# An encoder's feed-forward layers: gate and up by Strassen's seven block products, down in three parts

## The chip, the core and the metric

The kernel runs on one NeuronCore of a Trainium2 chip. PE (TensorE) multiplies matrices: it loads a 128x128 block of the stationary operand (PEld in the profile) and streams the columns of the moving operand through it into one of eight PSUM banks of 128 x 512 floats. DVE (VectorE), ACT (ScalarE) and POOL (GpSimd) work on tiles of 128 partitions; SP issues the DMA transfers from the chip's memory. Each engine takes its own instructions in order and waits for the others by semaphores. The metric is the device time of one execution in microseconds (us).

## The reference

The program is a two-layer encoder trunk on 512 tokens of width 1024, in float32. Layer 0 mixes tokens by neighbourhood attention and a bidirectional state-space scan, layer 1 by grouped-query attention. After each mixer stands a feed-forward network with hidden width 2816, and that is the part which the change touches:

```
def rms_norm(x, g):
    xf = x.astype(jnp.float32)
    y = xf * lax.rsqrt(jnp.mean(xf * xf, axis=-1, keepdims=True) + NORM_EPS)
    return (y * g.astype(jnp.float32)).astype(x.dtype)

def swiglu_ffn(x, norm_g, w13, w2):
    g, u = jnp.split(rms_norm(x, norm_g) @ w13, 2, axis=-1)
    return (jax.nn.silu(g) * u) @ w2
```

The result is added to x. The columns of w13 are 2816 for the gate g and 2816 for u (up); w2 leads back (down).

## The kernel before

The residual stream is kept transposed in eight tiles res[0..7] of 128 features x 512 tokens. A product in float32 quality is made of three fast ones: each operand is split into hi (a copy in the reduced type float32r, by ScalarE) and lo (the remainder t - hi, by VectorE), and mm3 (L150 to L155) adds lo*hi, hi*lo and hi*hi into one PSUM bank. So each 128x128 block of weights costs three matmuls of 512 columns, each with its own weight load.

load_w (L138 to L148) brings a weight tile of 128 x 1024: a DMA into a raw buffer (two, tag wr), a ScalarE copy to hi, a VectorE subtraction to lo (three buffers each, tags wh and wl). project (L166) multiplies one such tile with the eight input blocks: 24 matmuls. prep (L171) makes hi and lo of res[k] times the norm's gain.

ffn (L773 to L808) runs for each layer after its mixer. Hidden features are worked in HB = 22 blocks of 128. For each block there are two projections, gate into bank gp and up into bank up, 48 matmuls. The norm's factor rstd for each token isn't needed before the products are read: it is made from squares of res (L770), a column sum by two matmuls (sum_rows, L131) and a chain of ScalarE and VectorE operations (L189 to L200), and is multiplied on when the bank is read (L790, L792). silu is taken by ScalarE, the product g*s by VectorE (L793), and the hidden block is split again into hi and lo (L795, L796); all 22 hidden pairs stay in SBUF. Down then makes the eight output blocks one after the other, each from 22 hidden blocks in one bank, with weights in three loads (8, 8 and 6 blocks), and adds it to res (L806). In layer 1 the sum leaves by DMA (L808).

PSUM: seven of the eight banks are handed out in turn for ffn (turns["f"]), one is left for sums. Working tiles of 128 x 512 come from a pool of NSLOT = 12 slots, the split inputs from a pool of 16 (xgslot).

The order of instructions is made by a planner, which takes dependences and its own estimates of durations; only in the first mixer is a stretch of PE's order written out by hand (manual_schedule with PE alone).

## Time and profile before

| | |
|---|---|
| median of 3 runs | 1314.04 us (1313.2 to 1314.28) |
| the profiled execution | 1314.37 us, its span 1312.6 us |
| granted clock of PE, mean | 0.996 |
| busy share of the span | PE 98%, weight loads 81%, DVE 61%, ACT 46%, POOL 13% |
| feed-forward matmuls | nine groups of 352, 128x128 by 128x512 |
| DMA | 138.82 MB, mean 106 GB/s |

The span goes from the first to the last instruction of the profiled execution; its own time includes what lies around it. A row of the timeline gives the start in us, the duration, the engine, the line, the operation with output and inputs, and in brackets how long the engine had been idle before and what released it. Matmuls are pipelined, so their durations overlap: the distance between starts is what one costs. A group's row ends with its count, busy time and mean duration in ns, and the idle time of the engine before its instructions.

### The profile page before, as it was taken

How to read it: one execution, taken by the hardware profiler on the slowest of the kernel's cores; microseconds unless marked ns; L12 is line 12 of the kernel's file. 1: busy time of each engine (PE TensorE's matmuls, PEld its weight loads, DVE VectorE, ACT ScalarE, POOL GpSimd, SP SyncE). 2: the span in 40 equal slices, each digit the busy share in tenths (PEclk: the TensorE clock that was granted, in tenths of full speed). 3: DMA queues.
4: the chain of work that ended last, by engine and by line, in shares of the span. 5: the costliest groups of instructions: out<-in, count | busy, mean ns of one | idle time of the engine just before them, and what ended most of it. 6: DMA issues, size and time to landing. Idle time of an engine off the chain costs nothing.

```text
span 1312.6 us, 16744 instructions
## 1 busy us (share of the span) xinstructions
PE 1288.4 (98%) x6278; PEld 1062.6 (81%) x6278; DVE 805.2 (61%) x1262; ACT 604.0 (46%) x1023; POOL 167.5 (13%) x184
## 2 busy tenths in 40 slices
PE   9999999989999999999999999999999999999998
PEld 7777788867888888888888878778888888888887
DVE  6798798989684444444332578998864444443221
ACT  7676567866363333332233348777743222222220
POOL 5012011102000000000011325655100000000000
PEclk9999999989999999999999999999999999999999
DMA  7334443536333333323333343221132333333331
GB/s 239 97 98 153 128 132 114 177 93 191 105 111 97 97 96 96 97 97 104 94 100 103 112 105 89 81 65 33 49 113 96 97 97 96 96 97 106 107 118 55
DMA packets 49761, 138.82 MB, mean 106 GB/s; under 512 B 6736, under 2 KB 7888, under 8 KB 49680
## 3 DMA queue, kind: packets, MB, share of 16 engines
q1 hardware_dynamic: 49392, 137.23, 34.5%
q8 instruction: 49, 0.80, 0.2%
q10 hardware_dynamic: 288, 0.52, 0.1%
q14 instruction: 32, 0.26, 0.1%
HBM read 127.11 MB, written 2.23 MB: 99 GB/s over the span
## 4 chain that ended last, share of the span: by engine, by line
PE 81%; DVE 12%; ACT 4%; issue 2%; DMA 1%; SPq 0%; POOL 0%; DVEq 0%; ACTq 0%; POOLq 0%
PE fo L155 6%; PE fo L154 6%; PE fo L153 6%; PE fu L153 6%; PE fu L155 6%; PE fu L154 6%; PE fg L155 6%; PE fg L154 6%; PE fg L153 6%; PE g L153 2%; PE g L154 2%; PE g L155 2%; PE vps L271 2%; PE opt L968 1%; PE oA L153 1%
## 5 line engine op out<-in xcount | busy, mean ns | idle before, releaser
L155 PE MATMUL fg<-f_xh,wfg_h 128*128 128x512 f32 x352 | 137.0, 389 | 0.0
L154 PE MATMUL fg<-f_xl,wfg_h 128*128 128x512 f32 x352 | 137.0, 389 | 0.0
L153 PE MATMUL fu<-f_xh,wfu_l 128*128 128x512 f32 x352 | 136.9, 389 | 0.0
L154 PE MATMUL fu<-f_xl,wfu_h 128*128 128x512 f32 x352 | 136.9, 389 | 0.0
L155 PE MATMUL fu<-f_xh,wfu_h 128*128 128x512 f32 x352 | 136.9, 389 | 0.0
L153 PE MATMUL fo<-hh,wf_l 128*128 128x512 f32 x352 | 136.9, 389 | 0.0
L154 PE MATMUL fo<-hl,wf_h 128*128 128x512 f32 x352 | 136.9, 389 | 0.0
L155 PE MATMUL fo<-hh,wf_h 128*128 128x512 f32 x352 | 136.9, 389 | 0.0
L153 PE MATMUL fg<-f_xh,wfg_l 128*128 128x512 f32 x352 | 136.9, 389 | 0.0
L146 ACT ACTIVATE wf_h<-wf_r 128x1024 fp32r<-128x1024 f32 (+1 forms) x48 | 47.5, 990 | 180.3 <-PE fo L155 158.2
L147 DVE TENSOR_TENSOR wf_l<-wf_r,wf_h 128x1024 fp32r<-128x1024 f32 (+1 forms) x48 | 54.5, 1136 | 122.2 <-ACT wf_h L146 122.2
L146 ACT ACTIVATE wfg_h<-wfg_r 128x1024 fp32r<-128x1024 f32 x44 | 46.6, 1060 | 142.3 <-issue 127.3
L146 ACT ACTIVATE wfu_h<-wfu_r 128x1024 fp32r<-128x1024 f32 x44 | 46.7, 1061 | 135.5 <-PE fg L155 129.4
L792 DVE TENSOR_TENSOR g<-fu,fr_r 128x512 f32<-128x512 f32 x44 | 30.4, 691 | 124.6 <-PE fu L155 123.4
L790 DVE TENSOR_TENSOR g<-fg,fr_r 128x512 f32<-128x512 f32 x44 | 30.2, 691 | 87.7 <-PE fg L155 87.6
L155 PEld LDWEIGHTS fg<-f_xh,wfg_h 128*128 128x128 f32 x352 | 66.2, 188 | 13.9
L154 PEld LDWEIGHTS fo<-hl,wf_h 128*128 128x128 f32 x352 | 66.1, 188 | 13.8
L154 PEld LDWEIGHTS fu<-f_xl,wfu_h 128*128 128x128 f32 x352 | 66.2, 188 | 13.7
L153 PEld LDWEIGHTS fu<-f_xh,wfu_l 128*128 128x128 f32 x352 | 66.1, 188 | 13.7
L154 PEld LDWEIGHTS fg<-f_xl,wfg_h 128*128 128x128 f32 x352 | 66.0, 188 | 13.8
L153 PEld LDWEIGHTS fo<-hh,wf_l 128*128 128x128 f32 x352 | 66.1, 188 | 13.7
L155 PEld LDWEIGHTS fu<-f_xh,wfu_h 128*128 128x128 f32 x352 | 66.0, 188 | 13.7
(421 smaller groups left out, 2997.0 us busy)
## 6 DMA issues: line engine op xcount, KB each, us to landing
wfg_r<-in_w_fa SPq DMA_DIRECT2D x44, 512.0 KB, 3.5
wfu_r<-in_w_fa SPq DMA_DIRECT2D x44, 512.0 KB, 3.5
wf_r<-in_w_fb SPq DMA_DIRECT2D x32, 512.0 KB, 3.5
w_r<-in_w_ssd SPq DMA_DIRECT2D x24, 512.0 KB, 3.5
wo_r<-in_w_o SPq DMA_DIRECT2D x14, 512.0 KB, 3.6
wf_r<-in_w_fb SPq DMA_DIRECT2D x16, 384.0 KB, 3.2
nb<-in_nab SPq DMA_DIRECT2D x16, 256.0 KB, 2.9
ec<-ecumd SPq DMA_DIRECT2D x32, 128.0 KB, 3.0
```

Of the source, the lines that this page charges most:

```text
L146: A.activation(hi[:, 0:cols], raw, AF.Copy)
L147: (eng or V).tensor_tensor(lo[:, 0:cols], raw, f(hi)[:, 0:cols], ALU.subtract)
L153: T.matmul(ps, wl[:, a], xh[:, b], start=first, stop=False)
L154: T.matmul(ps, wh[:, a], xl[:, b], start=False, stop=False)
L155: T.matmul(ps, wh[:, a], xh[:, b], start=False, stop=last)
L271: T.matmul(vps[t], x_, w_[:, ws_], start=k + n == 0, stop=k == KB - 1 and n == 2)
L790: V.tensor_tensor(g, gp, rstd, ALU.mult)
L792: V.tensor_tensor(g, up, rstd, ALU.mult)
L968: T.transpose(pt[:, a * 256 + n * P:a * 256 + (n + 1) * P], pr[n][:, (2 * kp + a) * P:(2 * kp + a + 1) * P], ident)
```

## The change

Only ffn, load_w and mm3 change, and with ffn the constants. In ffn, the first NCL = 4 hidden blocks are made as before (gate_up), and the other 18 by Strassen's scheme in Winograd's form, class Fast. The weights of one hidden block are four blocks (gate and up; first and second half of the 1024 input features), the input four blocks (halves of the features; halves of the tokens, H = 256). Instead of eight products of such blocks there are seven, each of 4 k-tiles x 3 matmuls with 256 columns:

- sums of weight blocks: s1 = up first + up second, s2 = s1 - gate first, s0 = gate first - up first, s3 = gate second - s2; each is split into hi and lo (w0 to w6);
- sums of input blocks, made once per layer by forms, from the input that is multiplied by gain and rstd beforehand: t12 and t34, beside the plain x1 and xb;
- the products are added up in three half banks pa, pb, pc, which are read in between: after the first, third and fourth product by a ScalarE copy, after the fifth and sixth by a VectorE addition. c11 and c12 make the silu of the two token halves, h0 and h1 split the hidden block.

run(prev, nxt) writes one round: the seven products, of which the second (p3) belongs to the block before, mixed with the finish of that block and with the weights of the next.

Down is cut along the hidden blocks into 0 to 4 (after the four plain blocks), 4 to 12 (after block 13) and 12 to 22 (at the end); each part adds to res. So hidden tiles can be reused. The remainder of a weight tile can be put off (los). The whole of ffn stands in manual_schedule for PE, DVE and ACT: these three keep the written order; DMA issues do not.

```diff
-W2_SPLIT = (8, 8, 6)
+NCL, MID, UA = 4, 13, 1
...
+        def low():
+            (eng or V).tensor_tensor(lo[:, 0:cols], raw, f(hi)[:, 0:cols], ALU.subtract)
+        if los is None:
+            low()
+        else:
+            los.append(low)
...
+        H = S // 2
+        LOH, HIH = slice(0, H), slice(H, S)
+        LW, HW = slice(0, S), slice(S, 2 * S)
...
+        def copy(dst, src, scale=1.0):
+            A.activation(dst, src, AF.Copy, scale=scale)
+        def rest(lo, t, hi):
+            V.tensor_tensor(lo, t, f(hi), ALU.subtract)
+        def pair_of(name, tag, bufs, cols=S):
+            return [hlane(f"{name}{n}{layer}", f"{tag}{n}", bufs, F32R, cols) for n in "hl"]
+        hb = [None] * HB
+        def hidden(i):
+            mk = (lambda name: hlane(name, "h", 8, F32R)) if i < NCL or 12 <= i < 16 else xgslot
+            hb[i] = [mk(f"h{n}{layer}_{i}") for n in "hl"]
+            return hb[i]
+        def load_fa(n, los=None):
+            return load_w(w_fa[layer, n], 1024, f"wf{layer}_{n}", los=los)
+        x1, xb, t12, t34 = [], [None] * 4, [None] * 4, [None] * 4
+        def forms(k, r):
+            n = f"{layer}_{k}"
+            xa, xc, ta, tb = (slot(f"{m}{n}") for m in ("xa", "xc", "ta", "tb"))
+            V.scalar_tensor_tensor(xa, res[k], vc(gname, k), r, ALU.mult, ALU.mult)
+            if k % 2 == 0:
+                x1.append(pair_of(f"xa{n}", "xa", 2))
+            cut = part(x1[k // 2], slice(k % 2 * H, k % 2 * H + H))
+            copy(cut[0], xa[:, LOH])
+            V.scalar_tensor_tensor(xc, res[k + 4], vc(gname, k + 4), r, ALU.mult, ALU.mult)
+            b4, t1, t3 = xb[k], t12[k], t34[k] = [pair_of(f"{m}{n}", m, 4) for m in ("xb", "ta", "tb")]
+            copy(b4[0], xc)
+            yield
+            V.tensor_tensor(ta[:, LOH], xa[:, HIH], xa[:, LOH], ALU.subtract)
+            V.tensor_tensor(ta[:, HIH], xc[:, HIH], ta[:, LOH], ALU.subtract)
+            copy(t1[0], ta)
+            yield
+            V.tensor_tensor(tb[:, LOH], xc[:, HIH], xa[:, HIH], ALU.subtract)
+            V.tensor_tensor(tb[:, HIH], xc[:, LOH], ta[:, HIH], ALU.subtract)
+            copy(t3[0], tb)
+            yield
+            rest(cut[1], xa[:, LOH], cut[0])
+            rest(b4[1], xc, b4[0])
+            rest(t1[1], ta, t1[0])
+            rest(t3[1], tb, t3[0])
+        def product(ps, w, x, first=False):
+            for k in range(4):
+                if x is x1:
+                    xs, xc = x1[k // 2], slice(k % 2 * H, k % 2 * H + H)
+                else:
+                    xs, xc = x[0][k], x[1]
+                mm3(ps, w, k * P, xs, xc, first and k == 0, k == 3, skip=True)
+        class Fast:
+            def __init__(self, i):
+                self.i, self.n = i, f"{layer}_{i}"
+            def load(self):
+                n = self.n
+                self.gr = wsp.tile([P, 1024], F32, name=f"gr{n}", tag="wr", bufs=WR)
+                self.ur = hlane(f"ur{n}", "ur", 2, F32, 1024)
+                nc.sync.dma_start(self.gr, w_fa[layer, 2 * self.i])
+                nc.sync.dma_start(self.ur, w_fa[layer, 2 * self.i + 1])
+            def w0(self):
+                n, gr, ur = self.n, self.gr, self.ur
+                self.wg = [wsp.tile([P, 1024], F32R, name=f"g{m}{n}", tag=f"w{m}", bufs=b)
+                           for m, b in (("h", WH), ("l", WL))]
+                self.s = [slot(f"s{m}{n}") for m in range(4)]
+                copy(self.wg[0], gr)
+                V.tensor_tensor(self.s[0], gr[:, LW], ur[:, LW], ALU.subtract)
+                V.tensor_tensor(self.s[1], ur[:, LW], ur[:, HW], ALU.add)
+            def w1(self):
+                V.tensor_tensor(self.s[2], self.s[1], self.gr[:, LW], ALU.subtract)
+                rest(self.wg[1], self.gr, self.wg[0])
+            def w2(self):
+                V.tensor_tensor(self.s[3], self.gr[:, HW], self.s[2], ALU.subtract)
+                self.w32 = pair_of(f"sa{self.n}", "ss", 3, 1024)
+                copy(self.w32[0][:, LW], self.s[0])
+                copy(self.w32[0][:, HW], self.s[2])
+            def w3(self):
+                rest(self.w32[1][:, LW], self.s[0], self.w32[0][:, LW])
+                rest(self.w32[1][:, HW], self.s[2], self.w32[0][:, HW])
+            def w4(self):
+                self.w14 = pair_of(f"sb{self.n}", "ss", 3, 1024)
+                copy(self.w14[0][:, LW], self.s[1])
+                copy(self.w14[0][:, HW], self.s[3])
+                rest(self.w14[1][:, LW], self.s[1], self.w14[0][:, LW])
+            def w5(self):
+                rest(self.w14[1][:, HW], self.s[3], self.w14[0][:, HW])
+            def w6(self):
+                self.wu = pair_of(f"ua{self.n}", "ua", UA)
+                split(self.ur[:, HW], *self.wu)
+            def p1(self):
+                n = self.n
+                self.pa, self.pb, self.pc = (fbank(f"f{m}{n}")[:, 0:H] for m in "abc")
+                self.a, self.b, self.u, self.g = (slot(f"{m}{n}") for m in ("sa", "sb", "up", "sl"))
+                product(self.pa, part(self.wg, LW), x1, True)
+            def c11(self):
+                V.tensor_tensor(self.b[:, HIH], self.pc, self.a[:, LOH], ALU.add)
+                A.activation(self.g[:, LOH], self.b[:, HIH], AF.Silu)
+            def p3(self):
+                product(self.pa, part(self.w14, HW), (xb, HIH))
+            def c12(self):
+                A.activation(self.g[:, HIH], self.pa, AF.Silu)
+                V.tensor_tensor(self.u, self.u, self.g, ALU.mult)
+            def h0(self):
+                copy(hidden(self.i)[0], self.u)
+            def h1(self):
+                rest(hb[self.i][1], self.u, hb[self.i][0])
+            def run(self, prev, nxt):
+                if prev:
+                    prev.c11()
+                if nxt:
+                    nxt.w0()
+                self.p1()
+                copy(self.a[:, LOH], self.pa)
+                if nxt:
+                    nxt.w1()
+                if prev:
+                    prev.p3()
+                    prev.c12()
+                if nxt:
+                    nxt.w2()
+                product(self.pb, part(self.w32, LW), (t34, LOH), True)
+                copy(self.b[:, LOH], self.pb)
+                if prev:
+                    prev.h0()
+                if nxt:
+                    nxt.w3()
+                if prev:
+                    prev.h1()
+                product(self.pa, part(self.w32, HW), (t12, HIH))
+                copy(self.a[:, HIH], self.pa)
+                if nxt:
+                    nxt.w4()
+                product(self.pb, self.wu, (t34, HIH))
+                V.tensor_tensor(self.u[:, LOH], self.pb, self.a[:, HIH], ALU.add)
+                if nxt:
+                    nxt.w5()
+                    nxt.w6()
+                product(self.pa, part(self.w14, LW), (t12, LOH))
+                V.tensor_tensor(self.u[:, HIH], self.pa, self.b[:, LOH], ALU.add)
+                product(self.pc, part(self.wg, HW), (xb, LOH), True)
+        class Down:
+            def __init__(self, lo, hi, splits, final=False, wide=1):
+                self.banks, self.blocks, self.ws, self.wide = {}, [], [], wide
+                for o in range(0, KB, wide):
+                    k0 = lo
+                    for j, n in enumerate(splits):
+                        self.blocks.append((o, j, k0, n))
+                        k0 += n
+                self.lo, self.hi, self.final, self.last = lo, hi, final, len(splits) - 1
+            def load(self, upto, los=None):
+                while len(self.ws) < min(upto, len(self.blocks)):
+                    o, j, k0, n = self.blocks[len(self.ws)]
+                    src = [w_fb[layer, o + e, :, k0 * P:(k0 + n) * P] for e in range(self.wide)]
+                    self.ws.append(load_w(src, self.wide * n * P, f"wf2{layer}_{o}_{self.lo}_{j}", los=los))
+            def add(self, m, o, ks):
+                o0, j, k0, n = self.blocks[m]
+                if o not in self.banks:
+                    self.banks[o] = fbank(f"fo{layer}_{o}_{self.lo}")
+                for k in ks:
+                    mm3(self.banks[o], self.ws[m], ((o - o0) * n + k - k0) * P, hb[k], ALL,
+                        k == self.lo, k == self.hi - 1)
+                if k == self.hi - 1:
+                    V.tensor_tensor(res[o], res[o], self.banks[o], ALU.add)
+                    if self.final and layer == 1:
+                        nc.sync.dma_start(out[o], res[o])
+            def run(self, side, head=0):
+                for m, (o0, j, k0, n) in enumerate(self.blocks):
+                    for fn in side.get(m, ()):
+                        fn()
+                    self.load(m + 2)
+                    for o in range(o0, o0 + self.wide):
+                        self.add(m, o, range(k0, k0 + n - (m < head)))
+                    if m + 1 == head:
+                        for e in range(head * self.wide):
+                            self.add(e // self.wide, e, [self.hi - 1])
+        def gate_up(i, ws, xg, tick):
+            for n in range(2):
+                ps = fbank(f"f{'gu'[n]}{layer}_{i}")
+                order = [(k, p) for k in range(KB) for p in range(3)]
+                if i + n == 0:
+                    order = [(k, p) for k in range(KB) for p in (0, 2)] + [(k, 1) for k in range(KB)]
+                for m, (k, p) in enumerate(order):
+                    (wh, wl), (xh, xl) = ws[n], xg[k]
+                    T.matmul(ps, (wl if p == 0 else wh)[:, k * P:k * P + P], xl if p == 1 else xh,
+                             start=m == 0, stop=m == 23)
+                tick(n, ps)
+        with tc.manual_schedule(engines={mybir.EngineType.PE, mybir.EngineType.DVE, mybir.EngineType.Activation}):
+            ws = [load_fa(0), load_fa(1)]
+            xg, sq = [], []
+            for k in range(KB):
+                xg.append(prep(res[k], vc(gname, k), f"f{layer}{k}"))
+            for k in range(KB):
+                sq.append(slot(f"f{layer}_sq{k}"))
+                A.activation(sq[k], res[k], AF.Square)
+            for k in range(1, KB):
+                V.tensor_tensor(sq[0], sq[0], sq[k], ALU.add)
+            rstd = []
+            late = []
+            down0 = Down(0, NCL, (NCL,), wide=2)
+            fast = [Fast(i) for i in range(NCL, HB)]
+            def norm():
+                name = f"fr{layer}"
+                ps = bank(f"{name}_ss", "c")
+                sum_rows(ps, sq[0], name)
+                m, r, t = (slot(f"{name}_{n}") for n in "mrt")
+                ws.append(load_fa(3))
...
+                rstd.append(r)
+            def tick(i, n, ps):
+                los = []
+                m = 2 * i + 2 + n
+                if i + 1 < NCL:
+                    if m > 3:
+                        ws.append(load_fa(m, los))
+                    elif n == 0:
+                        ws.append(load_fa(m))
+                else:
+                    down0.load(1 + n, los)
+                if n == 0:
+                    if late:
+                        next(late[0])
+                    for lo in los:
+                        lo()
+                    for _ in late and late.pop():
+                        pass
+                    if i:
+                        gate(i, ps)
+                    else:
+                        first.append(ps)
+                    return
+                if i == 0:
+                    norm()
+                    gate(0, first[0])
+                g, s = banks.pop()
+                fm = forms(i, rstd[0])
+                next(fm)
+                for lo in los:
+                    lo()
+                def end():
+                    V.tensor_tensor(g, ps, rstd[0], ALU.mult)
+                    next(fm)
+                    yield
+                    V.tensor_tensor(g, g, s, ALU.mult)
+                    copy(hidden(i)[0], g)
+                    next(fm)
+                    rest(hb[i][1], g, hb[i][0])
+                    for _ in fm:
+                        pass
+                late.append(end())
+            def gate(i, ps):
+                g, s = slot(f"g{layer}_{i}"), slot(f"s{layer}_{i}")
+                V.tensor_tensor(g, ps, rstd[0], ALU.mult)
+                A.activation(s, g, AF.Silu)
+                banks.append((g, s))
+            banks, first = [], []
+            for i in range(NCL):
+                w2, ws[:] = ws[:2], ws[2:]
+                gate_up(i, w2, xg, lambda n, ps: tick(i, n, ps))
+            f0 = fast[0]
+            down0.run({0: [f0.load, lambda: [0 for _ in late.pop()]], 2: [f0.w0, f0.w1, f0.w2], 3: [f0.w3, f0.w4, f0.w5, f0.w6]}, 2)
+            fast[1].load()
+            prev = None
+            down1, down2 = Down(NCL, 12, (8,)), Down(12, HB, (5, 5), True)
+            for n, p in enumerate(fast):
+                nxt = fast[n + 1] if n + 1 < len(fast) else None
+                p.run(prev, nxt)
+                prev = p
+                end = [p.c11, p.p3, p.c12, p.h0, p.h1]
+                if p.i == MID:
+                    down1.load(1)
+                    down1.run({0: end})
+                    prev = None
+                if n + 2 < len(fast):
+                    fast[n + 2].load()
+            down2.load(2)
+            down2.run({0: end})
```

More of the change, by code (lines that the diff above doesn't have):

```diff
@@ L798, in ffn @@
-        for o in range(KB):
-            ps = fbank(f"fo{layer}_{o}")
-            k0 = 0
-            for j, n in enumerate(W2_SPLIT):
-                w = load_w(w_fb[layer, o, :, k0 * P:(k0 + n) * P], n * P, f"wf2{layer}_{o}_{j}")
-                for k in range(n):
-                    mm3(ps, w, k * P, hb[k0 + k], ALL, k0 + k == 0, k0 + k == HB - 1)
-                k0 += n
-            V.tensor_tensor(res[o], res[o], ps, ALU.add)
-            if layer == 1:
-                nc.sync.dma_start(out[o], res[o])
+        def copy(dst, src, scale=1.0):
+            A.activation(dst, src, AF.Copy, scale=scale)
@@ new lines, in rest, with split, part @@
+        def rest(lo, t, hi):
+            V.tensor_tensor(lo, t, f(hi), ALU.subtract)
+        def split(t, hi, lo):
+            copy(hi, t)
+            rest(lo, t, hi)
+        def pair_of(name, tag, bufs, cols=S):
+            return [hlane(f"{name}{n}{layer}", f"{tag}{n}", bufs, F32R, cols) for n in "hl"]
+        def part(p, cols):
+            return [t[:, cols] for t in p]
+        hb = [None] * HB
[3 more added lines that the diff above has]
+            return hb[i]
@@ new lines, in product, with weights @@
+        def product(ps, w, x, first=False):
[43 more added lines that the diff above has]
+                split(self.ur[:, HW], *self.wu)
+            def weights(self):
+                for w in (self.w0, self.w1, self.w2, self.w3, self.w4, self.w5, self.w6):
+                    w()
+            def p1(self):
[49 more added lines that the diff above has]
+                product(self.pc, part(self.wg, HW), (xb, LOH), True)
```

36 lines of the change are left out of this document (12 added, 24 removed).

## The prediction

> **What bounds the kernel now.** I read the engine totals and the chain of waits on the page first, then the busy time in the stretches of the first feed-forward layer, then single matmuls in order of time.
>
> ```profile
> span 1312.6 us, 16744 instructions
> PE 1288.4 (98%) x6278; PEld 1062.6 (81%) x6278; DVE 805.2 (61%) x1262; ACT 604.0 (46%) x1023; POOL 167.5 (13%) x184
> ...
> PE 81%; DVE 12%; ACT 4%; issue 2%; DMA 1%; SPq 0%; POOL 0%; DVEq 0%; ACTq 0%; POOLq 0%
> ...
> 370.00:611.00 241.00, 240.65 (x1062) 198.96 (x1062) 121.09 (x149) 78.76 (x99) 0.00 (x0) 1.00 0.32 100
> 611.00:731.50 120.50, 120.50 (x533) 99.83 (x532) 39.65 (x43) 34.36 (x41) 8.98 (x6) 1.00 0.33 97
> ```
>
> The last two rows are gate and up (370 to 611) and down (611 to 731.5) of layer 0; the columns after the length are PE, weight loads, DVE, ACT, POOL, then granted clock (1.00), DMA share and GB/s. TensorE never rests there, VectorE is busy for half of gate and up. So a matmul less is time less, as long as VectorE can feed the new form.
>
> The duration of one matmul misleads: matmuls overlap. What counts is the distance between starts.
>
> ```profile
> 370.50 0.39 PE L153 MATMUL fg<-f_xh,wfg_l 128*128 128x512 f32 x1
> ...
> 375.94 0.39 PE L153 MATMUL fu<-f_xh,wfu_l 128*128 128x512 f32 x1
> ...
> 480.69 0.69 DVE L792 TENSOR_TENSOR g<-fu,fr_r 128x512 f32<-128x512 f32 x1 [3.14 <-PE fu L155]
> ...
> 491.57 0.69 DVE L792 TENSOR_TENSOR g<-fu,fr_r 128x512 f32<-128x512 f32 x1 [3.14 <-PE fu L155]
> ```
>
> The first two rows are 24 matmuls apart: 5.44 / 24 = 0.2267 us for 512 columns. The other two show the same step of two successive hidden blocks: **10.88 us for a block** of 48 such matmuls.
>
> **Part 1, the products.** Of 22 hidden blocks per layer four keep their 48 matmuls of 512 columns. Eighteen become 7 products x 4 k-tiles x 3 matmuls = 84 of 256 columns: 7/8 of the columns, in 84 instructions for 48. The trace has 256-column matmuls with a fresh 128x128 weight load each, in the odd mixer and in the neighbourhood attention.
>
> ```profile
> 755.12 0.28 PE L1037 MATMUL gv<-wgvl,o_xh 128*128 128x256 f32 x1
> 755.24 0.28 PE L1038 MATMUL gv<-wgvh,o_xl 128*128 128x256 f32 x1
> ...
> 757.88 0.28 PE L1039 MATMUL gv<-wgvh,o_xh 128*128 128x256 f32 x1
> ...
> 761.07 0.39 PE L1037 MATMUL gv<-wgvl,o_xh 128*128 128x256 f32 x1 [0.24 <-ACT gvv L1041]
> 761.29 0.28 PE L1038 MATMUL gv<-wgvh,o_xl 128*128 128x256 f32 x1
> ...
> 763.91 0.28 PE L1039 MATMUL gv<-wgvh,o_xh 128*128 128x256 f32 x1
> ...
> 65.06 0.28 PE L392 MATMUL nsc<-kl,q 128*128 128x256 f32 x1
> ...
> 65.41 0.28 PE L392 MATMUL nsc<-kh,q 128*128 128x256 f32 x1
> ```
>
> 755.12 to 757.88 is 23 steps, 0.1200 each; 761.29 to 763.91 is 22 steps, 0.1191; 65.06 to 65.41 three, 0.117. I take 0.1195, with 0.117 and 0.120 as ends. Two halves then cost 0.239 for one whole of 0.2267: a fixed 12 ns per matmul eats 5% of the 12.5%. A block: 84 x 0.1195 = **10.04 us**, 0.84 less than 10.88 (1.05 and 0.80 at the ends). Times 36 blocks in two layers: **-30.2 us** (-37.8 to -28.8). Down keeps its 528 matmuls of 512 columns per layer: 0.
>
> By the Trainium skill (TensorE: Matmul & The Clock Gate, Back-to-back issue gap) a stream of weight loads and matmuls is paced by both, at some 81 ns for 128 columns and 131 ns for 512; an estimate on the straight line between gives 98 ns for 256, by which 84 short ones would take 31% longer than 48 long ones. The trace does not agree: 227 ns for 512 and 120 ns for 256.
>
> **Part 2, the weight combinations.** Each fast block adds VectorE and ScalarE work. Counted in one call of run: VectorE has eleven operations of 512 columns (four sums of weights, five remainders of 512, the product u*g, the remainder of the hidden block), one remainder of 1024 and three additions of 256 out of PSUM. ScalarE has one copy of 1024, six of 512, and five operations of 256.
>
> ```profile
> 482.03 1.22 DVE L147 TENSOR_TENSOR wfg_l<-wfg_r,wfg_h 128x1024 fp32r<-128x1024 f32 x1
> 483.16 0.69 DVE L796 TENSOR_TENSOR hl<-g,hh 128x512 fp32r<-128x512 f32 x1
> ...
> 252.02 0.69 DVE L677 TENSOR_TENSOR gs_ql<-gsq,gs_qh 128x512 fp32r<-128x512 f32 x1
> 252.62 0.69 DVE L570 TENSOR_TENSOR cbl<-cb,cstt 128x512 f32<-128x512 f32 x1
> 253.22 0.68 DVE L570 TENSOR_TENSOR cbg<-cb,cstt 128x512 f32<-128x512 f32 x1
> ...
> 776.31 0.42 DVE L1046 TENSOR_TENSOR gvt<-gvv,gvt 128x256 fp32r<-128x256 f32 x1 [2.71 <-ACT gvt L1045]
> ...
> L146 ACT ACTIVATE wfg_h<-wfg_r 128x1024 fp32r<-128x1024 f32 x44 | 46.6, 1060 | 142.3 <-issue 127.3 <-PE fu L155 12.6 <-PE oA L155 1.7
> L795 ACT ACTIVATE hh<-g 128x512 fp32r<-128x512 f32 x44 | 27.9, 633 | 20.7 <-DVE g L793 20.6
> L1041 ACT ACTIVATE gvv<-gv,ort 128x256 f32<-128x256 f32 x4 | 1.8, 464 | 2.2 <-PE gv L1039 2.2
> ```
>
> VectorE starts follow each other by 0.60 for 512 columns (252.02, 252.62, 253.22) and 1.13 for 1024 (482.03 to 483.16), less than their durations, so 512 columns are worth 0.53; the one of 256 lasts 0.42, and its start-to-start distance, 0.60 less half of 0.53, would be 0.33. So 11 x 0.60 + 1.13 + 3 x 0.33 = **8.7 us in a round of 10.04**; at full durations, 11 x 0.69 + 1.22 + 3 x 0.42 = 10.1, the upper bound. ScalarE: 1.06 + 6 x 0.63 + 5 x 0.46 = 7.1.
>
> Busy time under the round is not enough, since all three engines now keep the written order. So I walked one round from the end of the last product (t = 0), PE doing seven products of 12 x 0.1195 = 1.43 us: p1, the previous block's p3, and five more. VectorE: c11, both sums of w0, w1 until 3.5; c12 waits for p3 (2.87) and its silu and ends at 4.2; s3 and the two remainders of w3 until 6.0; the hidden remainder until 6.6; w4's remainder waits for the ScalarE copy behind the one that reads the fourth product (5.74 + 0.46 + 0.63) and ends at 7.5; the rest ends at 9.4. It then waits for the last product: 0.7 us to spare. What PE asks of the others: the copy of b before the fifth product (done 4.9, asked 5.74), the copy of a's half before the sixth (6.3, asked 7.17), the addition into u before the next p3 (9.4, asked 11.5). The weights of the next block are a whole round early, and a bank is reused over two rounds later. So **0 us** per round, hidden by matmuls; without that cover each late accumulator costs what the 761.07 row shows, 0.24 of waiting and a first step of 0.22 for 0.12: 0.34.
>
> DMA: the same 1 MB per block, in 10.04 instead of 10.88 us. Buffers of block n+2 come free in round n-1, so a landing of 3.5 us has a round to spare:
>
> ```profile
> wfg_r<-in_w_fa SPq DMA_DIRECT2D x44, 512.0 KB, 3.5
> ```
>
> **Part 3, four blocks of the old kind and what is made beside them.** Each layer starts with squares and the norm, then forms makes the input sums. The norm's chain:
>
> ```profile
> 383.57 0.69 ACT L189 ACTIVATE fr_m<-fr_ss,epst 128x512 f32<-128x512 f32 x1 [0.60 <-PE fr_ss L136]
> ...
> 387.48 0.69 DVE L200 TENSOR_TENSOR fr_r<-fr_r,fr_t 128x512 f32<-128x512 f32 x1
> ...
> 264.13 0.74 DVE L518 SCALAR_TENSOR_TENSOR grp<-g,vect,grp 128x510 f32<-128x510 f32 x1
> 264.79 0.74 DVE L174 SCALAR_TENSOR_TENSOR so_xl<-yn,vect,so_xh 128x512 fp32r<-128x512 f32 x1
> ```
>
> From 383.57 to 388.17 it takes 4.6. The sum of squares stands on PE behind two projections of 5.44, so the norm is ready 10.9 + 0.5 + 4.6 = 16.0 after the layer's first matmul. VectorE has waited and now owes, in order: gate(0) 0.60, two fused products at 0.66, 0.60 and two halves at 0.33, a weight remainder 1.13, 0.60, two halves, 0.60, 0.33 and three of 0.60, gate(1) 0.60: 8.9, until 24.9. Behind it on ScalarE the silu (0.62), then the copy of weight 5 (1.06), then its remainder (1.13): 27.7, with some ten hand-overs between engines of about 0.1 (the idle 0.60 above is the longest) 28.7. The up projection of block 2 asks at 5 x 5.44 + 0.5 = 27.7. I take **1.1 us late** per layer (0 to 3); its queue, all later projections, moves along, and each of these then finds its weights 0.3 to 1.2 early, since VectorE owes only 9.5 of 10.88 per block.
>
> **Part 4, down in three parts.** Two more additions into each res, 16 x 0.69 per layer on VectorE, beside matmuls. The 24 loads per layer become 8 of half size, 8 and 16, in SP's order between the gate and up loads. In the first part the last block's raw buffer either comes free with the remainder before it or only after s3 of the first fast block; then load, copy and remainder (3.5 + 1.06 + 1.13) end up to 3.6 after PE asks. I take 0.4 per layer (0 to 3.6). The middle part has only two weight buffers, since the next fast block holds the third; copy and remainder (2.2) fit in a block of 24 x 0.2267 = 5.44. In the last part 15 matmuls, 3.4, cover 1.4.
>
> **Part 5, the seams.** Written order could keep work of the next stage from coming early. Now:
>
> ```profile
> 715.90 0.85 ACT L146 ACTIVATE wf_h<-wf_r 128x768 fp32r<-128x768 f32 x1 [2.97 <-PE fo L155]
> ...
> 716.77 1.28 ACT L812 ACT_TABLE_LOAD   x1
> ...
> 730.44 0.39 PE L155 MATMUL fo<-hh,wf_h 128*128 128x512 f32 x1
> 730.66 0.39 PE L153 MATMUL kpa<-o_xh,wka_l 128*128 128x512 f32 x1
> ```
>
> ScalarE goes to the next layer's table right after its last weight copy, 14 us before PE does (730.66), so it is in program order already; afterwards the last copy is some 7 us ahead, enough for table and first weights. I take 1.0 for all four seams (0 to 9: copy, remainder and first preparation in series at three of them, about 3 each).
>
> **Sum**, against the profiled execution's 1314.37 (span 1312.6, 1.8 around it; the median of the runs is 1314.04, the same within 0.03%): -30.2 + 2 x 1.1 + 2 x 0.4 + 1.0 = -26.2: **1288**.
>
> **Rivals.**
>
> *VectorE becomes the bound.* If starts follow by durations, the round holds 10.1 plus some eight hops of 0.05: 10.5. It decides from 10.04 on. For: six waits on ScalarE in a round. Against: 0.60 is measured between unrelated operations. 1314.4 - 36 x 0.38 + 4 = 1305.
>
> *Accumulators handed back late; slower.* PE adds into banks that ScalarE or VectorE has read in between, at four products of seven. A read queued behind a copy that waits for VectorE stalls PE at 0.34 each. The margin is 0.84 - 4 / 36 = 0.73 a round, so from three such waits (1.02) it is slower: 36 x 0.18 + 4 = +10.5, 1325. For: margins of 0.8 in the walk, one VectorE lag of 2 us uses them. Against: a stalled PE gives VectorE time.
>
> *A higher fixed cost per short matmul.* Break-even is 10.88 / 84 = 0.1295. By that, 1318. Against: no run of steps above 0.120; for: the longest has 24 in a row, here thousands follow. This is the skill's pacing rule as a mechanism of this kernel.
>
> *The starts eat the gain.* Upper ends of parts 3 to 5: 2 x 6.6 + 9 = 22 for the 4 taken: 1306. For: margins of 0.3; against: they would all have to fail.
>
> **Chances and range.** Forecast 0.68 (own range 1277 to 1299), VectorE 0.11, starts 0.06, late accumulators 0.11, fixed cost 0.04. A measurement here tells about 0.2% (2.6 us) from no change; within that lie the edges of three rivals, 0.04. Faster is 0.68 + 0.11 + 0.06 less 0.02: 0.83; slower 0.13. The range goes from the 0.117 end without stalls (1277) over VectorE and starts to 1312; it leaves out the slower cases.
>
> **What would show it.** Right: starts of 256-column matmuls 0.119 to 0.120 apart, 10.0 us between equal steps of fast blocks, VectorE at 85 to 90% there, no PE waits at p3, the fifth and the sixth product; one PE wait of about 1 us at the third up projection. Wrong: rounds over 10.5, PE waiting on ScalarE copies of a or b, or gaps at the seams.

## The result and the profile after

The changed kernel takes **1291.99 us** (median of 4 runs, 1291.68 to 1293.63) against 1313.62 for the kernel before (4 runs, 1311.97 to 1314.28): a ratio of **0.984**, 95% interval 0.9823 to 0.9857. That is 21.6 us less, where 26.2 were forecast. The profiled execution of after took 1293.63 with a span of 1291.8, so the spans (1312.6 before) differ by 20.8, and the account below is made in spans.

The page of the kernel after, its totals and the chain of waits:

```profile
span 1291.8 us, 20184 instructions
PE 1260.6 (98%) x7574; PEld 1101.0 (85%) x7574; DVE 1008.6 (78%) x1706; ACT 722.1 (56%) x1351; POOL 164.9 (13%) x184
...
PE 68%; DVE 19%; ACT 7%; issue 4%; DMA 1%; POOL 0%; SPq 0%; DVEq 0%; ACTq 0%; POOLq 0%
```

There are 1296 more matmuls, and PE is busy for 27.8 us less. VectorE goes from 61% to 78%, and its part of the chain that ended last from 12% to 19%. The busy time in stretches of layer 0 after says where (the columns are the stretch, its length, then PE, weight loads, DVE, ACT, POOL, granted clock, DMA share, GB/s):

```profile
369.40:416.00 46.60, 44.46 (x195) 36.23 (x194) 42.17 (x68) 26.55 (x41) 0.00 (x0) 1.00 0.25 80
416.00:439.30 23.30, 22.07 (x97) 17.94 (x96) 22.02 (x35) 11.23 (x16) 0.00 (x0) 1.00 0.30 93
439.30:540.10 100.80, 100.80 (x841) 100.77 (x840) 90.78 (x150) 59.43 (x118) 0.00 (x0) 1.00 0.34 109
540.10:583.70 43.60, 43.60 (x195) 36.09 (x194) 14.78 (x16) 9.40 (x10) 0.00 (x0) 1.00 0.33 100
```

The rows are the four blocks of the old kind, the first part of down, ten fast blocks, and the middle part of down; the other eight fast blocks and the last part of down follow. PE never rests in the fast blocks nor in the middle part. It rests 2.14 us in the old blocks and 1.23 in the first part of down, and those are the two stretches in which VectorE is busy all but 4.4 and 1.3 us.

The steps of the fast blocks, from the timeline of PE after:

```profile
458.04 0.28 PE L159 MATMUL fa<-xa_0h,gl 128*128 128x256 f32 x1
...
468.12 0.28 PE L159 MATMUL fa<-xa_0h,gl 128*128 128x256 f32 x1
468.24 0.28 PE L160 MATMUL fa<-xa_0l,gh 128*128 128x256 f32 x1
...
478.20 0.28 PE L159 MATMUL fa<-xa_0h,gl 128*128 128x256 f32 x1
```

The same step comes back every **10.08 us** (458.04, 468.12, 478.20): 84 starts 0.120 apart. Before, the block took 10.88.

What PE still waits for in the feed-forward layers of after (total us, times, the longest), and where:

```profile
PE fo L159 <- DVE wf_l L148: 2.5, 2, 1.3
PE fr_ss L135 <- DVE fr_ql L134: 2.2, 2, 1.1
PE fu L1006 <- DVE wf_l L148: 2.0, 2, 1.1
```

```profile
369.37 0.39 PE L1006 MATMUL fg<-f_xh,wf_l 128*128 128x512 f32 x1
...
381.49 0.47 PE L135 MATMUL fr_ss<-fr_ql,ones_r 128*128 128x512 f32 x1 [1.08 <-DVE fr_ql L134]
...
399.57 0.47 PE L1006 MATMUL fu<-f_xh,wf_l 128*128 128x512 f32 x1 [1.06 <-DVE wf_l L148]
...
416.01 0.39 PE L159 MATMUL fo<-hh,wf_l 128*128 128x512 f32 x1
...
433.75 0.50 PE L159 MATMUL fo<-hh,wf_l 128*128 128x512 f32 x1 [1.23 <-DVE wf_l L148]
...
439.32 0.28 PE L159 MATMUL fa<-xa_0h,gl 128*128 128x256 f32 x1
```

There are three waits per layer, each once: the sum of squares, the third up projection, the last weight of the first part of down. No accumulator of a product is in the list.

**The account.** Fast blocks: 36 x (10.08 - 10.88) = -28.8. Old blocks and first part of down: 369.37 to 439.32 is 69.95. Their 288 matmuls of 512 columns are 65.3 by the 0.2267 of before, and the sum of squares added some 1.1 there (the layer's 360.16 of before, less 1584 x 0.2267), so without new waits it would be 66.4: +3.55, and +3.67 in layer 1, together +7.2. Middle and last part of down: 0, they take 192 and 240 times 0.2267. What lies between and around the layers: +0.75. The sum is -20.85, and the spans say -20.8.

### The profile page after: what moved, and what is told of

The parts are those of the page before. It is cut to its first block, busy times and chain, and to the rows that moved or that the text cites. A ratio compares the mean times of both kernels' runs of the same rounds, so it can differ in the third digit from the quotient of the medians.

```text
span 1291.8 us, 20184 instructions
## 1 busy us (share of the span) xinstructions
PE 1260.6 (98%) x7574; PEld 1101.0 (85%) x7574; DVE 1008.6 (78%) x1706; ACT 722.1 (56%) x1351; POOL 164.9 (13%) x184
## 4 chain that ended last, share of the span: by engine, by line
PE 68%; DVE 19%; ACT 7%; issue 4%; DMA 1%; POOL 0%; SPq 0%; DVEq 0%; ACTq 0%; POOLq 0%
PE fa L161 5%; PE fa L160 5%; PE fa L159 5%; PE fo L159 5%; PE fo L160 5%; PE fo L161 5%; PE fb L161 3%; PE fb L160 3%; PE fb L159 3%; PE vps L277 2%; PE oA L159 1%; PE opt L1271 1%; PE oA L160 1%; PE oA L161 1%; PE fc L161 1%
## 5 line engine op out<-in xcount | busy, mean ns | idle before, releaser
L161 PEld LDWEIGHTS fo<-hh,wf_h 128*128 128x128 f32 x352 | 66.1, 188 | 13.8
L159 PE MATMUL g<-n_xh,w_l 128*128 128x512 f32 x192 | 76.6, 399 | 0.0
L161 PE MATMUL g<-n_xh,w_h 128*128 128x512 f32 x192 | 75.3, 392 | 0.0
L160 PE MATMUL g<-n_xl,w_h 128*128 128x512 f32 x192 | 75.2, 392 | 0.0
L1262 POOL TENSOR_SCALAR op<-op,osum 128x512 f32<-128x512 f32 x64 | 45.5, 719 | 55.2 <-DVE osum L1261 38.3
L1260 ACT ACTIVATE op<-os,omx 128x512 f32<-128x512 f32 x64 | 43.6, 686 | 14.8 <-DVE omx L1258 12.6
L1275 DVE TENSOR_TENSOR opt<-opt,opt 128x512 fp32r<-128x512 f32 x64 | 43.6, 683 | 6.9 <-ACT opt L1274 6.2
L1274 ACT ACTIVATE opt<-opt 128x512 fp32r<-128x512 f32 x64 | 38.0, 599 | 18.8 <-PE opt L1271 18.3
L1258 DVE TENSOR_REDUCE omx<-os 128x1 f32<-128x512 f32 x64 | 42.1, 681 | 4.5 <-PE os L1256 4.3
L793 DVE TENSOR_TENSOR gl<-gr,gh 128x1024 fp32r<-128x1024 f32 x36 | 43.9, 1219 | 0.0
```

Of the source, the lines that this page charges most:

```text
L159: T.matmul(ps, wl[:, a], xh[:, b], start=first, stop=False, skip_group_check=skip)
L160: T.matmul(ps, wh[:, a], xl[:, b], start=False, stop=False, skip_group_check=skip)
L161: T.matmul(ps, wh[:, a], xh[:, b], start=False, stop=last, skip_group_check=skip)
L793: V.tensor_tensor(lo, t, f(hi), ALU.subtract)
L1258: V.tensor_reduce(mx, sps, AX.X, ALU.max, negate=True)
L1260: A.activation(p_, sps, AF.Exp, bias=mx, accum_out=sums)
```

## The experiments

The first four kernels, run beside the kernel before at 1314.78, ask whether the forecast's two limits are what they seem: the price of a short matmul and VectorE's margin in a round.

### The kernel before, with its gate and up matmuls halved

```diff
-            project(gp, w_fa[layer, 2 * i], xg, f"wfg{layer}_{i}")
-            project(up, w_fa[layer, 2 * i + 1], xg, f"wfu{layer}_{i}")
+            for ps, n, tag in ((gp, 2 * i, "g"), (up, 2 * i + 1, "u")):
+                w = load_w(w_fa[layer, n], 1024, f"wf{tag}{layer}_{i}")
+                for half in (slice(0, 256), slice(256, 512)):
+                    for k in range(KB):
+                        mm3(ps[:, half], w, k * P, xg[k], half, k == 0, k == KB - 1)
```

> The kernel before, with each of the 24 matmuls of a gate or up projection cut into two of 256 columns (first all for tokens 0 to 255, then all for 256 to 511). Same columns, same sums, twice the matmuls and weight loads. Theory (a short matmul costs 0.120 us between starts where a long one costs 0.2267): 44 blocks x (96 x 0.120 - 10.88) = +28.2, so 1341.8 against 1313.6. Rival (only columns count): 1313.6, no change.

Measured: 1342.76 (1339.97 to 1343.29), ratio 1.0208 (1.0193 to 1.0223). Two starts from the timeline of PE in this kernel, ten matmuls apart:

```profile
479.78 0.28 PE L153 MATMUL fg<-f_xh,wfg_l 128*128 128x256 f32 x1
...
480.98 0.28 PE L154 MATMUL fg<-f_xl,wfg_h 128*128 128x256 f32 x1
```

That is 0.120 each, 0.240 for two halves where the whole took 0.2267. Times 2112 matmuls of gate and up in both layers the difference is 28.2 us; 28.0 were measured. So the price of a short matmul is there without Strassen's scheme, and it makes a column 5.9% dearer: 7/8 of the columns take 92.6% of the time, as 10.08 to 10.88 does.

### One more, and three more, VectorE operations in each round

```diff
                 V.tensor_tensor(self.s[0], gr[:, LW], ur[:, LW], ALU.subtract)
+                for _ in range(n):        # n = 1, n = 3
+                    V.tensor_tensor(self.s[0], gr[:, LW], ur[:, LW], ALU.subtract)
```

> The changed kernel with one more VectorE operation of 512 columns in each fast block's weights (s0 = gate - up is computed twice, 0.60 us). Theory (PE's 84 starts pace the round of 10.08, VectorE waits some 0.7 us for the last product): hidden, 0 to +2, 1292 to 1294. Rival (VectorE is the bound already): +0.60 x 36 = +21.6, 1313.6.

> The same with three more such operations (1.80 us a round). Theory: 0.7 of it is hidden, 1.1 x 36 = +40, 1332. If VectorE had far more room than 0.7: 1292. If it were the bound already: +65, 1357.

Measured: one more 1299.91 (1298.23 to 1301.43), ratio 0.9886 (0.9871 to 0.9901); three more 1338.61 (1337.24 to 1339.3), ratio 1.018 (1.0164 to 1.0195). The same step of successive rounds in the timeline of PE, first with one more, then with three more; below these a wait of PE and the busy time in a stretch of fast blocks with three more:

```profile
470.43 0.28 PE L159 MATMUL fa<-xa_0h,gl 128*128 128x256 f32 x1
...
480.51 0.28 PE L159 MATMUL fa<-xa_0h,gl 128*128 128x256 f32 x1
```

```profile
475.35 0.28 PE L159 MATMUL fa<-xa_0h,gl 128*128 128x256 f32 x1
...
486.40 0.28 PE L159 MATMUL fa<-xa_0h,gl 128*128 128x256 f32 x1
```

```profile
PE fb L159 <- ACT sb L790: 17.1, 30, 1.5
```

```profile
447.00:537.00 90.00, 85.21 (x681) 82.16 (x680) 88.66 (x146) 49.26 (x98) 0.00 (x0) 1.00 0.29 95
```

With one more, the round stays at 10.08: the margin holds 0.60. With three more it is 11.05, VectorE is busy for 88.66 of 90 us, and PE waits for copies of the accumulator b, just as a late VectorE was said to show. So the margin lies between one operation and three. The first ten rounds of a layer take 11.18 each on average in this kernel, the other eight 10.95; over both layers that is 35.9 of the 43.6 us by which its span (1335.4) is longer than the changed kernel's, and the first part of down has another 5.8. The total with one more is some 6 us above what was expected, though. By spans (1297.5 against 1291.8) it is 5.7: some 1.3 stand in the four stretches of rounds (about 0.3 once in each), 3.1 at the first part of down, whose wait grows to 2.0 at the longest, and 1.3 ahead of layer 0. That last stretch is the same in both kernels; in the repetition of the changed kernel below it is 2.1 longer than in the first trace (layer 0 begins at 371.44 and at 369.37), so this part is scatter.

### The fifth product left out

```diff
-                product(self.pb, self.wu, (t34, HIH))
```

> The changed kernel with the fifth product of each fast block left out (up second half times t34's second half; so up of the first 256 tokens lacks that term), with all VectorE and ScalarE work kept. PE then asks 72 x 0.120 = 8.64 a round. Theory: VectorE, busy 9.1 of 10.08 with some waits that remain, becomes the bound at about 9.4: -0.7 x 36 = -25, 1267. Rival (VectorE has far more room, PE alone sets the round): -1.44 x 36 = -52, 1240. Rival (VectorE is the bound already): 1292.

Measured: 1269.99 (1267.97 to 1270.47), ratio 0.966 (0.9644 to 0.9676). The timeline of PE and the busy time in a stretch of fast blocks of this kernel:

```profile
475.93 0.28 PE L159 MATMUL fa<-xa_0h,gl 128*128 128x256 f32 x1
...
485.29 0.28 PE L159 MATMUL fa<-xa_0h,gl 128*128 128x256 f32 x1
```

```profile
447.00:520.00 73.00, 69.21 (x563) 67.59 (x562) 70.69 (x118) 46.01 (x94) 0.00 (x0) 1.00 0.39 114
```

PE would need 72 x 0.120 = 8.64 a round; it takes **9.36**, with VectorE busy for 97% of the stretch. So 9.36 is VectorE's own round, with the few waits that it keeps, and both other kernels fit it: 9.36 + 0.60 = 9.96 is under PE's 10.08 (one more costs nothing in a round), and 9.36 + 3 x 0.60 = 11.16 is over it (11.05 measured between two steps). By this the change has some 0.72 us to spare in a round.

### The three waits at the start, one by one and together

Next come the 7.2 us of the starts. My theory had three separate waits, each with its own cause in the written order; the rival had one backlog of VectorE, which shows up wherever relief isn't given. Each of three kernels mends one: weight 5 is loaded and split right behind weight 4; the weight sums of the first fast block are put behind the last weight of down; squares and their additions are mixed with the first input tiles. A fourth does all three. They ran beside the kernel before at 1314.6.

```diff
-                    if m > 3:
+                    if m == 4:
+                        ws.extend([load_fa(4, los), load_fa(5, los)])
+                    elif m > 5:
                         ws.append(load_fa(m, los))
```

> The changed kernel with weight 5 (up of plain block 2) copied and split right behind weight 4, ahead of the forms and the second gate on VectorE, and not behind them. Theory (the wait of 1.06 and 0.93 at the third up projection comes from VectorE's order): about -1.2 per layer, -2.4, 1289.6. Rival (the backlog stays, so the next projection waits instead): 1292.

```diff
-  2: [f0.w0, f0.w1, f0.w2], 3: [f0.w3, f0.w4, f0.w5, f0.w6]}, 2)
+  3: [f0.w0, f0.w1, f0.w2, f0.w3, f0.w4, f0.w5, f0.w6]}, 2)
```

> The changed kernel with w0, w1 and w2 of the first fast block written after the last weight load of the first down part, not before it. Theory (the wait of 1.23 and 1.29 there comes from this weight's copy and remainder standing behind w0 to w2 and four additions into res): -1.2 to -1.4 per layer, about -2.5, 1289.5. Rival (its raw buffer comes free too late, as the prediction had it): 1292, or more where the first fast product then waits for its weights.

```diff
                 xg.append(prep(res[k], vc(gname, k), f"f{layer}{k}"))
-            for k in range(KB):
                 sq.append(slot(f"f{layer}_sq{k}"))
                 A.activation(sq[k], res[k], AF.Square)
-            for k in range(1, KB):
-                V.tensor_tensor(sq[0], sq[0], sq[k], ALU.add)
+                if k:
+                    V.tensor_tensor(sq[0], sq[0], sq[k], ALU.add)
```

> The changed kernel with each square and its addition written right behind the preparation of its block, not all squares after all preparations. Theory (the sum of squares is 1.08 late at PE since its seven additions run one after the other, 0.75 apart, behind everything else): 0.7 to 1.1 per layer, about -1.8, 1290.2. Rival (VectorE is full there in any order): 1292.

> The three together. Theory (three separate waits): the sum, -5 to -7, 1285 to 1287. Rival (they share one backlog of VectorE): no more than the best of them alone, 1289 or 1290.

| kernel | median us | ratio (95%) | old blocks, layer 0 / 1 | first part of down |
|---|---|---|---|---|
| weight 5 early | 1294.4 | 0.9844 (0.9826 to 0.9862) | 45.80 / 45.81 | 24.04 / 24.08 |
| down first | 1296.6 | 0.9856 (0.9839 to 0.9872) | 46.62 in layer 0 | 21.91 / 21.98 |
| squares early | 1301.06 | 0.989 (0.9872 to 0.9908) | 48.74 / 48.68 | 23.31 in layer 0 |
| all three | 1301.05 | 0.9892 (0.9877 to 0.9907) | 47.94 in layer 0 | 22.65 in layer 0 |

None beats the change's 0.984. The medians also hold the scatter ahead of layer 0, which begins anywhere from 368.10 to 372.59 us in the traces of all these kernels. The stages alone are free of it: from the first gate projection to the end of the tenth fast block the changed kernel takes 170.75 us in either layer, and again in its repetition below. Against that, over both layers, the four stand at -0.2, +1.4, +4.2 and +6.8 us. In the waits of PE with weight 5 early, the up projection's wait falls from 2.0 to 0.4 and that of down grows from 2.5 to 3.4:

```profile
PE fo L159 <- DVE wf_l L148: 3.4, 4, 1.3
...
PE fu L1006 <- DVE wf_l L148: 0.4, 2, 0.2
```

With down first, the first part of down takes 21.91, which is 96 x 0.2267 within 0.15: its wait is gone. But the ten fast blocks behind it take 102.90 instead of 100.80, and PE now waits for an accumulator there:

```profile
419.21 0.39 PE L159 MATMUL fo<-hh,wf_l 128*128 128x512 f32 x1
...
441.12 0.28 PE L159 MATMUL fa<-xa_0h,gl 128*128 128x256 f32 x1
...
544.02 0.40 PE L159 MATMUL fo<-hh,wf_l 128*128 128x512 f32 x1
```

```profile
PE fb L159 <- ACT sb L790: 3.7, 2, 1.9
```

With squares early, the wait for the sum is gone and the first gate projection waits for its input tiles instead (3.0 for remainders, 1.6 for copies, over both layers):

```profile
PE fg L1006 <- DVE f_xl L180: 3.0, 4, 0.8
...
PE fg L1006 <- ACT f_xh L179: 1.6, 4, 0.4
```

My theory fell. A wait that is mended comes back at the next point at which VectorE's backlog meets PE, in three of the four kernels dearer.

### The order of VectorE and ScalarE left to the planner; and GpSimd's help

One backlog may be too much work, or work in the wrong order. The change writes out the order of three engines; this kernel writes out PE's alone, and the planner orders the other two. Beside it run the changed kernel again, and two kernels that take work from VectorE instead: GpSimd makes the four remainders of each input sum, and in the second also adds half of the squares. The kernel before took 1315.17 here.

```diff
-        with tc.manual_schedule(engines={mybir.EngineType.PE, mybir.EngineType.DVE, mybir.EngineType.Activation}):
+        with tc.manual_schedule(engines={mybir.EngineType.PE}):
```

> The changed kernel with the written order kept for PE alone; VectorE's and ScalarE's order is left to the planner. Theory (the written order of VectorE is tight but good: rounds of 10.08 with no wait of PE): the planner can lose by putting the remainders elsewhere, 1293 to 1305. Rival (the written order causes the waits at the start of the layer): below 1290.

> The changed kernel again, for comparison on the same chip: ratio 0.983 to 0.985 as before, that is 1293 where the kernel before takes 1314.6.

Measured: the planner's order **1289.97** (1286.64 to 1290.89), ratio **0.9806** (0.979 to 0.9823); the changed kernel beside it 1295.98 (1292.61 to 1296.26), ratio 0.9848 (0.983 to 0.9867). My theory, that the planner can only lose, fell. The bounds of the stages in the timeline of PE with the planner's order (those of the changed kernel, 369.37, 416.01 and 439.32, stand above, and its repetition has the same 46.64 and 23.32 between them):

```profile
371.20 0.39 PE L1006 MATMUL fg<-f_xh,wf_l 128*128 128x512 f32 x1
...
416.43 0.39 PE L159 MATMUL fo<-hh,wf_l 128*128 128x512 f32 x1
...
438.19 0.28 PE L159 MATMUL fa<-xa_0h,gl 128*128 128x256 f32 x1
```

The old blocks go from 46.64 to 45.23, the first part of down from 23.32 to 21.76, which is 96 x 0.2267 without a wait. That is 2.97 in layer 0, and the stages of layer 1 give as much; the fast rounds are the same in both. So 5.9 of the 6.0 us between the two medians are the starts. VectorE has nearly the same work up to the first fast product (62.73 of 66.99 us busy in 101 operations, 64.23 of 69.96 in 102 in the changed kernel); what differs is the order. Whether VectorE's order or ScalarE's counts for more is not shown, since both were left to the planner. Remainders of weights in the timeline of VectorE, in the repetition of the changed kernel (its layer begins at 371.44, the planner's at 371.20), and with the planner's order:

```profile
387.02 0.69 DVE L1035 TENSOR_TENSOR fr_t<-fr_t,fr_m 128x512 f32<-128x512 f32 x1 [2.46 <-ACT fr_t L1034]
...
392.67 1.22 DVE L148 TENSOR_TENSOR wf_l<-wf_r,wf_h 128x1024 fp32r<-128x1024 f32 x1 [0.26 <-ACT wf_h L146]
```

```profile
384.31 1.23 DVE L148 TENSOR_TENSOR wf_l<-wf_r,wf_h 128x1024 fp32r<-128x1024 f32 x1 [1.23 <-ACT wf_h L146]
...
431.06 1.22 DVE L148 TENSOR_TENSOR wf_l<-wf_r,wf_h 128x1024 fp32r<-128x1024 f32 x1
```

In the written order VectorE stands idle for 2.46 us in the norm's chain, and weight 4's remainder is queued behind that chain. The planner makes it before, while VectorE has nothing else to do (384.31 against 392.67). The remainder of the last weight of down's first part, 431.06, begins 59.86 after the layer's start, where the changed kernel has 63.11 (432.48 less 369.37; the row stands below, at part 4).

```diff
-            rest(cut[1], xa[:, LOH], cut[0])
-            rest(b4[1], xc, b4[0])
-            rest(t1[1], ta, t1[0])
-            rest(t3[1], tb, t3[0])
+            for lo, t, hi in ((cut[1], xa[:, LOH], cut[0]), (b4[1], xc, b4[0]),
+                              (t1[1], ta, t1[0]), (t3[1], tb, t3[0])):
+                G.tensor_tensor(lo, t, f(hi), ALU.subtract)
...
-            for k in range(1, KB):                               # the second kernel alone
-                V.tensor_tensor(sq[0], sq[0], sq[k], ALU.add)
+            for k in range(1, 4):
+                G.tensor_tensor(sq[0], sq[0], sq[k], ALU.add)
+            for k in range(5, KB):
+                V.tensor_tensor(sq[4], sq[4], sq[k], ALU.add)
+            V.tensor_tensor(sq[0], sq[0], sq[4], ALU.add)
```

> The changed kernel with the four remainders of forms (2.1 us per plain block on VectorE) given to GpSimd, which rests there. Theory (the waits of the plain blocks and the first down part are one VectorE backlog; its order only moves them, taking work off removes them): the waits at the third up projection (1.1) and at the last weight of the first down part (1.3) vanish, about -2.5 per layer, -5, ratio 0.980. Rival (GpSimd slows VectorE while it works, or the waits have separate causes): ratio 0.984 or above.

> The same, and the first four squares are added up on GpSimd while VectorE adds up the other four. Theory: the wait at the sum of squares (1.1) goes too, about -3.5 per layer, -7, ratio 0.979. Rival: as for the one before; or GpSimd's additions are so slow that the sum comes later.

Measured: the remainders on GpSimd 1297.39 (1295.51 to 1300.16), ratio 0.9869 (0.9852 to 0.9886); with the squares 1304.94 (1302.71 to 1307.04), ratio 0.9925 (0.9912 to 0.9939). Neither is a gain: from the first gate projection to the end of the tenth fast block, both layers together, they take 2.3 and 9.6 us more than the changed kernel. Two operations from the timeline of VectorE with the remainders on GpSimd, GpSimd's own at that time, and the first of the two in the changed kernel:

```profile
388.64 1.40 DVE L830 TENSOR_TENSOR ta<-xc,ta 128x256 f32<-128x256 f32 x1
...
391.11 1.77 DVE L1073 TENSOR_TENSOR g<-g,s 128x512 f32<-128x512 f32 x1
```

```profile
388.43 1.33 POOL L838 TENSOR_TENSOR xb_0l<-xc,xb_0h 128x512 fp32r<-128x512 f32 x1
390.79 1.54 POOL L838 TENSOR_TENSOR ta_0l<-ta,ta_0h 128x512 fp32r<-128x512 f32 x1 [1.03 <-ACT ta_0h L790]
```

```profile
389.91 0.43 DVE L830 TENSOR_TENSOR ta<-xc,ta 128x256 f32<-128x256 f32 x1
```

VectorE's operation takes 1.40 instead of 0.43 and ends at 390.04, after GpSimd's has ended at 389.76; the next such pair costs 1.77 instead of 0.69. What VectorE is relieved of (0.33 and three times 0.60 a block) comes back as time in which it is blocked: up to the first fast product it has 16 operations fewer and is busy for 65.67 us instead of 64.23. The Trainium skill (SBUF — State Buffer, "SBUF: two separate sides") states it as a lock on a shared pair of ports, between GpSimd and a VectorE operation with two inputs from SBUF, which the one that starts first holds for its whole instruction; these rows agree.

With the squares too, the wait for the sum of squares is gone and the first input tiles come late by 4.8 us over both layers, as with squares early.

## Why the prediction was right, and where it was off

The forecast was 1288, inside a range from 1277 to 1312; 1292 was measured. The likeliest case came true by its mechanism, and of the 5.4 us between the forecast sum and the one by spans (-26.2 and -20.85) nearly all lies in two terms.

**Part 1, the products.** Right in kind: 84 short matmuls replace 48 long ones at a higher price per column. The spacing was 0.1200 in thousands of matmuls, the upper end of what was given and not the 0.1195 taken: 0.80 a block, -28.8 for -30.2. The 1.4 us are the choice between two rows of before (0.1200 over 23 steps, 0.1191 over 22). The halved kernel shows that the price belongs to the short matmul. The rival of a higher fixed cost (0.1295) is out. The pacing of the Trainium skill (TensorE: Matmul & The Clock Gate, Back-to-back issue gap), by which the estimate was 98 ns for 256 columns beside 131 for 512, is not what these float32r pairs show: 120 and 227.

**Part 2, the round of VectorE.** Right in kind and in size. In the walk VectorE ended at 9.4 us and had 0.7 to spare; with a product left out its own round measures 9.36. That the two meet within 0.04 is partly luck, since the walk's steps were rounded to 0.1. In the changed kernel VectorE's idle time in a round is mostly one wait, before the sum that makes c11:

```profile
458.24 0.43 DVE L908 TENSOR_TENSOR sb<-fc,sa 128x256 f32<-128x256 f32 x1 [0.82 <-PE fc L161]
```

That is the wait for the last product. VectorE's share in ten rounds is 90.78 of 100.80, the upper end of the 85 to 90% named. Since the margin is some 0.72, the rival in which VectorE becomes the bound was two operations of 512 columns a round away, and so was the slower one by late accumulators: three more operations make both come true, with waits on copies of b and 1338.61. What spoke against them was the size of the margin alone.

**Part 3, the old blocks.** The third up projection waits 1.06 and starts slower, 1.2 in all for the 1.1 forecast (the forecast's own walk, 28.7 less 27.7, gives 1.0). What was not foreseen is the sum of squares, which the forecast took over from before as it was. There PE waited 0.35 us for it, as this row of before shows:

```profile
382.80 0.50 PE L135 MATMUL fr_ss<-fr_ql,ones_r 128*128 128x512 f32 x1 [0.35 <-DVE fr_ql L134]
```

Here it waits 1.08: the squares' additions on VectorE stand in one block behind the eight input tiles (seven of them, 0.80 apart). That is 0.7 a layer.

**Part 4, the first part of down.** Here a term was mis-sized and its cause wrong. I took 0.4 and blamed the raw buffer; it was 1.55 and 1.63 in the two layers (23.31 and 23.39 less 96 x 0.2267), and the weight was late by VectorE's queue. That queue in the timeline of VectorE after, ahead of the last weight, and below it the copy of that weight in the timeline of ScalarE:

```profile
425.28 1.22 DVE L148 TENSOR_TENSOR wf_l<-wf_r,wf_h 128x1024 fp32r<-128x1024 f32 x1
426.42 2.47 DVE L983 TENSOR_TENSOR xr<-xr,fo 128x512 f32<-128x512 f32 x4
428.81 0.68 DVE L867 TENSOR_TENSOR s<-gr,ur 128x512 f32<-128x512 f32 x1
...
432.48 1.22 DVE L148 TENSOR_TENSOR wf_l<-wf_r,wf_h 128x1024 fp32r<-128x1024 f32 x1
```

```profile
430.86 0.63 ACT L790 ACTIVATE sa_4h<-s 128x512 fp32r<-128x512 f32 x1 [0.70 <-DVE s L871]
431.40 1.04 ACT L146 ACTIVATE wf_h<-wf_r 128x1024 fp32r<-128x1024 f32 x1
```

None of VectorE's rows has idle time ahead of it. Four additions into res (2.47) and the sums and one remainder of the first fast block's weights (428.81 to 432.48) stand ahead of the last remainder, which ends at 433.70; PE had asked at 432.52. ScalarE's copy of this weight is late with it: it comes behind the copy of a sum that VectorE makes late (430.86), and ends as the remainder begins. The raw buffer was not the limit. It came free with the remainder ahead of it (426.50), and the two transfers, issued at 426.53 and 426.91, had landed by 429.9; copied and split at once (1.04 + 1.22), the weight would have been there at 432.2, by this estimate 0.3 before PE asked. The forecast had put those additions "beside matmuls" at no cost and had not walked VectorE through this stretch as it did through the round. Parts 3 and 4 together were 3.0 for both layers and measured 7.2. Of that the planner's order takes back 5.9, so most of it is the order and not the amount of work. The middle and the last part cost nothing, as forecast.

**Part 5, the seams.** 1.0 forecast, 0.75 by the account, but this agreement is luck. The stretch ahead of layer 0 is 1.1 shorter, and that is scatter: in the repetition of the changed kernel it is 0.9 longer than before. The stretch between the layers is 1.9 longer (2.4 in the repetition), about twice the forecast; some 0.8 of it lie at the first projection behind the layer. The rest is spread over the odd mixer, and I did not settle it.

## What to carry to other kernels

A scheme that trades matmuls for additions pays by the start-to-start distance of the matmuls that it really issues (0.240 for two halves against 0.2267) and holds as long as the engine that makes the sums stays under the round: walk that engine through the steady round, and just as closely through the start and each change of stage, where its backlog decides. When one engine is nearly full for 70 us, mending one wait moves it to the next; look for what could be done while that engine is idle, and try the planner's order of that engine before writing one out. GpSimd was no relief here for a VectorE whose operations read two tiles of SBUF.

## What was not expected of the hardware

A 128x128 float32r matmul with its own weight load does not get cheaper in proportion to its columns: 0.2267 us for 512 and 0.1200 for 256. A straight line through the two is 0.0133 + columns x 0.00042, but two lengths don't test it. It doesn't reach down to 128 columns in the matmuls that this program has there, in plain float32; these, in layer 0's mixer of the kernel after, start 0.112 apart, where the line would give 0.067:

```profile
169.17 2.84 PE L595 MATMUL st<-xw,btok 128*128 128x128 f32 x24
```

Weight loads are busy for 100.77 of 100.80 us in the ten fast blocks and for 36.09 of 43.60 in the middle part of down, so they may set this least distance; no run here shows it. A second halving, to 128 columns, would by these rows hardly shorten a matmul. That is an estimate, and the type of these rows is another.

A VectorE subtraction of two tiles of SBUF went from 0.43 to 1.40 us when it met a GpSimd operation of 1.33. And the version that beats both kernels is the change with PE's order alone written out: 0.9806 (0.979 to 0.9823) of the time before.
